# Where attention's token statistics, head rows and weight sums stand in the order of a two-layer decoder kernel

## The chip, the cores and the metric

The kernel runs on one core of a Trainium2 chip. A core has five engines with queues of their own: TensorE (PE, with weight loads shown as PEld), VectorE (DVE), ScalarE (ACT), GpSimd (POOL) and SyncE (SP, which here only issues transfers). They work side by side and wait for each other by semaphores. The metric is the device time of one execution in microseconds (us). The time of the kernel before is the median of three executions, 1449.32 us, of 1448.95 to 1450.97.

## The reference

Two layers over 528 tokens (16 learned ones and 512 of input) of width 1024. Layer 0 is an attention with forget gates, layer 1 a gated linear recurrence; each is followed by a gated feed-forward part with a short convolution. Cut to what matters here:

```python
def rms_norm(x, gain):
    return x * lax.rsqrt(jnp.mean(x * x, axis=-1, keepdims=True) + EPS) * gain

def fox_attention(h, norm_g, w_in, b_f, q_gain, k_gain, w_out):
    xn = rms_norm(h, norm_g)
    q, k, v, f_logit, o_gate = jnp.split(xn @ w_in, [D, 2 * D, 3 * D, 3 * D + H], axis=-1)
    q = rms_norm(q.reshape(B, L, H, hd), q_gain) * (hd ** -0.5)
    k = rms_norm(k.reshape(B, L, H, hd), k_gain)
    c = jnp.cumsum(jax.nn.log_sigmoid(f_logit + b_f), axis=1).transpose(0, 2, 1)
    # scores s = q.k + c_t - c_s, causal; softmax; o = p @ v
    o = o * jax.nn.sigmoid(o_gate)
    return o @ w_out

def conv_ffn(h, norm_g, w_gate, w_up, conv_w, conv_b, w_down):
    xn = rms_norm(h, norm_g)
    a = conv_b + causal_conv3(xn @ w_gate, conv_w)
    return (jax.nn.silu(a) * (xn @ w_up)) @ w_down
```

There are 16 heads of 64, so 8 pairs of heads, each pair 128 rows wide.

## The kernel before, in words

**Number form.** Activations and weights are kept as a sum of two parts, `hi` and `lo`. A product of 128 x 128 weights with 264 tokens is three matmuls, written by `proj_unit` at L250, L253 and L254. `weights` (L184) loads a weight tile into `raw` (two buffers), ACT makes `hi` (L200) and DVE `lo` (L126), with three buffers each. The factor 1/rms of a token is not multiplied into the activations: it is worked out beside the products and put on their results.

**Token statistics.** ACT squares the eight tiles of `h` and DVE adds them up to `ss` (L314, L318). `token_stats` (L345) lets PE sum `ss` over the partitions (L350, L352), and DVE takes the reciprocal root (`am`, `rsqn`, `rst`). In attention the sums are also needed as rows: PE makes them at L430, DVE copies them to `ssr` (L431), four transfers turn them into `et` (L434). `spread_rs` (L363) makes the row `rsb`, the factor for all partitions. All this is written ahead of the first products (L424 to L436).

**Stages of attention.** `stage_a(p)` makes q and k of pair p: 4 x 24 matmuls. For pair 0 the four products run side by side in the banks "p", "p", "c", "d"; other pairs take "p" banks, of which there are two (`bank`, L173; there are four "s" banks, one "c", one "d"). ACT squares and scales the results (L535, L536), PE sums the squares per head (L544), ACT copies them to `strow` (L545), four transfers bring them to `am2` (L549), where DVE adds `et` (L552), takes the reciprocal root and sends it back as `rows` (L559). `ssr`, `strow` and the forget logits `zr` are tiles of one tag with one buffer. `stage_n` multiplies the rows in (L573, L574), splits q and k and packs them into a slot (L600). `stage_f` makes the forget logits (L452, L453) and `forget` turns them into running sums on DVE, with a prefix over partitions on PE (L483); `decays` sends them into the slots (L612). `stage_v` makes values of two pairs with `values` (L268: L284, L291, L301). `stage_l` takes the log-sum-exp of the heads of a pair, one after the other, with `lse` (L730): five groups of scores (L744, L745, L747), the maxima on DVE (L757), exponentials on ACT, then a row that PE transposes (L779), DVE copies (L781) and transfers put into the slot (L784, L785). `stage_t` makes the attention itself. `stage_g` makes the output gate, `stage_p` a first part of the output projection.

**Order.** Stages are Python generators that yield a cost in us; `weave` interleaves them in proportion, `take` runs a part of one. The loop over p from -3 to 7 at L684 lays stage a of pair p+3, n of p+2, l of p+1 and t of p side by side. The order in which the instructions are written is not the order of issue: `tile.TileContext(nc, schedule_with_timeline_sim=True)` (L1432) sets the order of each engine at build time. `after(ins, prev)` (L94) adds an edge that keeps one instruction behind another in that order. On the chip each engine takes its queue in the order so fixed.

**Weight sums.** Most of the feed-forward part multiplies 2 x 2 blocks with seven products, for which sums of weight blocks are needed. `make_sums` (L211) is a generator: each step starts one or two sums, each by a load on SP and an adding transfer on POOL (L225, L226), into pieces of 512 columns of three shared tiles, two called `two` (four pieces each) and one called `one` (three). Six steps are taken in the output projection ahead of the feed-forward part (L727, L1096), then three in each `seven` (L1194, L1201, L1207). `plain` (L1239) makes the first pair of hidden tiles without sums.

Of the kernel before, what the change touches and what calls it, by code (L numbers as in the profile page):

```python
# [21 lines left out]
P = 128  # L22
D = 1024
KT = D // P
T = 528
# [57 lines left out]
class Builder:  # L83
# [158 lines left out]
    def proj_unit(self, ps, units, x, t0, tn, prev=None):  # L242
# [4 lines left out]
        for hi, lo, n in units:  # L247
            for i in range(n):
                xh, xl = (y[:, t0 : t0 + tn] for y in x[k])
                ins = mm(ps, hi[:, i, :], xh, start=k == 0, stop=False)  # L250
                if k == 0 and prev is not None:
                    self.after(ins, prev)
                mm(ps, hi[:, i, :], xl, start=False, stop=False)  # L253
                mm(ps, lo[:, i, :], xh, start=False, stop=k == total - 1)  # L254
                k += 1
                if k % 2 == 0:
                    yield 0.66
# [86 lines left out]

    def token_stats(self, segs, last=False, bank=None):  # L345

        nc = self.nc
        ps = (bank or self.misc)()[:, :12].rearrange("p (t c) -> p t c", c=2)
        for t, (t0, _, i0, _) in enumerate(segs):
            nc.tensor.matmul(ps[:, t, :], self.ss[:, t0 - i0 : t0 - i0 + P], self.onesd, start=True, stop=True)  # L350
        if last:
            nc.tensor.matmul(ps[:16, 5, :], self.ss[:, 512:528], self.onesd, start=True, stop=True)  # L352
        am = self.cp.tile([P, 6], F32, name="am", tag="am", bufs=2)
# [22 lines left out]
    def fox(self, ctx):  # L376
# [47 lines left out]
        start = partial(self.bank, "s")  # L424
        am, rs = self.token_stats(SEG0, True, start)
        et = sp.tile([64, 33], F32, name="et")
        ssr = s2.tile([2, T], F32, name="ssr", tag="strow", bufs=1)
        for t0, tn in full:
            sr = start()
            mm(sr[:2, :tn], self.onesd, self.ss[:, t0 : t0 + tn], start=True, stop=True)  # L430
            nc.vector.tensor_copy(ssr[:, t0 : t0 + tn], sr[:2, :tn])  # L431
        for g in range(4):
            t0, tn = full[g % 2]
            nc.sync.dma_start(et[16 * g : 16 * g + 16, :], ssr[:, t0 : t0 + tn].rearrange("r (j c) -> r j c", c=33))  # L434
        nc.vector.tensor_scalar(et, et, EPS, EPS, ALU.add, ALU.mult)
        self.spread_rs(rs, SEG0, start)  # L436
        rcol = [0, 1, 2, 3, 5]
# [71 lines left out]
        def stage_a(p):  # L509
# [16 lines left out]
            for w_, nm in ((0, "q"), (1, "k")):  # L526
# [4 lines left out]
                for i, (t0, tn) in enumerate(full):  # L531
                    ps = banks[i] if banks else bank()
                    if not banks:
# [11 lines left out]
            nc.scalar.copy(strow, pst[:, :264])  # L545
            yield 0.9
            am2 = self.tiny.tile([64, 33], F32, name="am2", tag="am2")
            for g in range(4):
# [68 lines left out]
        def stage_l(p):  # L617
            if p == 0:
                decays(0)
            for d in packs[p]:  # L620
                yield from self.lse(d, s2, identb, maskq)

# [61 lines left out]
        for p in range(-3, NPAIR):  # L684
            fill, cost = [], 0.0
            if p % 2 and 0 <= p + 1 < NPAIR:
                fill.append(vgen[p + 1])
                cost += half if p > 0 else 2 * half
            if p + 3 < NPAIR:
                fill.append(stage_a(p + 3))  # L690
# [29 lines left out]
        for i, m in enumerate([NEARLY, *range(NEARLY), *range(NEARLY + 1, KT)]):  # L720
# [4 lines left out]
            for step, _ in enumerate(out_proj(m, 6 if m < NEARLY else 0, KT, res)):  # L725
                if i > 1 and step == 0:
                    next(self.making)  # L727
# [111 lines left out]
    def hgrn(self, ctx):  # L839
# [254 lines left out]
        for m in range(KT):  # L1094
            if m > 1:
                next(self.making)  # L1096
# [10 lines left out]
    def ffn(self, ctx, layer, a0, o0):  # L1107
# [131 lines left out]
        def plain(j, out):  # L1239

            A, t = new_pair("A"), new_pair("t")[:, :, :n]
            for m in range(2):
                wg = [block(a[f"gu{layer}"][2 * j + m, 0, k]) for k in range(2)]
                for t0, tn in ga:
                    ps = self.bank("sp"[m])[:, :tn]
# [191 lines left out]
```

## Time and profile before

| | us |
|---|---|
| median of three executions | 1449.32 |
| profiled execution, whole | 1452.92 |
| its span, first to last instruction | 1451.1 |
| PE busy in it | 1420.7 |
| DVE busy | 1010.1 |
| ACT busy | 724.3 |

The difference of whole and span, 1.8 us, lies around the span. Times in a row of the timeline are the start from the beginning of the span and the length; a row may stand for several instructions (x10). What stands in brackets is how long the engine was idle before it, and what ended that. "PEclk" is the clock granted to PE, as a share of full speed: a matmul at a lower clock counts as busy and takes longer.

The first 350 us are attention, up to about 1100 us follow the first feed-forward part and the recurrence, the rest is the second feed-forward part.

### The profile page before, as it was taken

To read this page: it belongs to the slowest core of one execution; us is meant where nothing else is said; L and a number is where in the kernel's file an instruction comes from. 1 tells how busy PE (TensorE), PEld (TensorE's weight loads), DVE (VectorE), ACT (ScalarE), POOL (GpSimd) and SP (SyncE) were. 2 spreads that over 40 slices of the span, in tenths; PEclk is the share of its full clock that TensorE was granted. 3 is DMA by queue.
4 is the path that set the end of the run, shared out by engine and by line. 5 is a ranking of instruction groups with operands and counts; after the bars stand their busy time and mean duration, and the time that the engine had idled before them with its cause. 6 is when DMAs were issued, how large, how long until landed. Compare 5 with 4: busy or idle time off the path is not lost.

```text
span 1451.1 us, 29767 instructions
## 1 busy us (share of the span) xinstructions
PE 1420.7 (98%) x11368; PEld 1339.2 (92%) x11368; DVE 1010.1 (70%) x2282; ACT 724.3 (50%) x1528; POOL 164.3 (11%) x273
## 2 busy tenths in 40 slices
PE   7999999999899999999999999999999999999998
PEld 6898888899899999999999999999999899999997
DVE  6545455775698886767775667677656987777774
ACT  5356554663566554554543224333435665555551
POOL 4000000001012222221000000000100222221100
PEclk9999999999999999999999999999999999999999
DMA  4424344335659898886322202222643899989833
GB/s 161 120 63 134 76 124 123 89 99 150 182 138 232 231 238 203 205 214 165 97 61 87 88 2 88 61 72 74 170 122 84 206 256 220 237 214 222 203 90 101
DMA packets 105463, 206.90 MB, mean 143 GB/s; under 512 B 14168, under 2 KB 18008, under 8 KB 105320
## 3 DMA queue, kind: packets, MB, share of 16 engines
q1 hardware_dynamic: 82280, 163.05, 36.9%
q0 software_dynamic: 23040, 41.95, 17.5%
q8 instruction: 89, 1.46, 0.4%
q14 instruction: 54, 0.44, 0.1%
HBM read 168.53 MB, written 2.10 MB: 118 GB/s over the span
## 4 chain that ended last, share of the span: by engine, by line
PE 91%; DMA 4%; DVE 2%; ACT 2%; SPq 1%; issue 1%; DVEq 0%; ACTq 0%
PE pss L250 7%; PE pss L254 7%; PE pss L253 7%; PE psp L250 7%; PE psp L253 7%; PE psp L254 7%; PE psp L301 6%; PE psp L1183 5%; PE psp L1184 5%; PE psp L1185 5%; PE psd L1183 3%; PE psd L1184 3%; PE psd L1185 3%; PE psc L816 2%; PE pss L974 1%; PE psc L1183 1%
## 5 line engine op out<-in xcount | busy, mean ns | idle before, releaser
L126 DVE TENSOR_TENSOR lo<-raw,hi 128x512 fp32r<-128x512 f32 (+2 forms) x322 | 252.8, 790 | 79.8 <-ACT hi L1160 39.9
L250 PE MATMUL psp<-xhi,hi 128*128 128x264 f32 (+2 forms) x784 | 228.1, 292 | 6.2 <-ACT xhi L326 6.2
L253 PE MATMUL psp<-xlo,hi 128*128 128x264 f32 (+2 forms) x784 | 226.4, 289 | 0.0
L254 PE MATMUL psp<-xhi,lo 128*128 128x264 f32 (+2 forms) x784 | 225.9, 289 | 0.0
L1160 ACT CAST hi<-raw 128x512 fp32r<-128x512 f32 (+1 forms) x232 | 139.2, 604 | 170.4 <-PE pss L253 58.6
L253 PE MATMUL pss<-room,hi 128*128 128x264 f32 (+2 forms) x532 | 169.7, 320 | 0.0
L254 PE MATMUL pss<-room,lo 128*128 128x264 f32 (+2 forms) x532 | 168.8, 320 | 0.0
L250 PE MATMUL pss<-room,hi 128*128 128x264 f32 (+2 forms) x532 | 168.1, 320 | 0.0
L250 PEld LDWEIGHTS psp<-xhi,hi 128*128 128x128 f32 x784 | 149.9, 192 | 9.8 <-ACT xhi L326 6.2
L200 ACT CAST hi<-raw 128x1024 fp32r<-128x1024 f32 (+2 forms) x86 | 83.1, 968 | 145.0 <-PE psp L253 63.9
L253 PEld LDWEIGHTS psp<-xlo,hi 128*128 128x128 f32 x784 | 149.7, 191 | 2.2 <-issue 2.1
L254 PEld LDWEIGHTS psp<-xhi,lo 128*128 128x128 f32 x784 | 149.2, 191 | 2.0 <-issue 1.9
L1183 PE MATMUL psp<-xhi,hi 128*128 128x264 f32 (+1 forms) x480 | 136.4, 284 | 3.4 <-ACT hi L1160 2.7
L1185 PE MATMUL psp<-xhi,lo 128*128 128x264 f32 (+1 forms) x480 | 136.2, 284 | 0.9 <-DVE lo L126 0.9
L1184 PE MATMUL psp<-xlo,hi 128*128 128x264 f32 (+1 forms) x480 | 135.7, 283 | 0.0
L1160 ACT CAST hi<-two 128x512 fp32r<-128x512 f32 x118 | 72.9, 619 | 84.5 <-PE psd L1184 33.0
L254 PEld LDWEIGHTS pss<-room,lo 128*128 128x128 f32 x532 | 100.1, 189 | 6.3
L253 PEld LDWEIGHTS pss<-room,hi 128*128 128x128 f32 x532 | 100.2, 188 | 5.2
L250 PEld LDWEIGHTS pss<-room,hi 128*128 128x128 f32 x532 | 99.5, 188 | 4.2
L1307 DVE TENSOR_TENSOR h<-h,pss 128x264 f32<-128x264 f32 (+2 forms) x145 | 73.6, 508 | 36.3 <-PE pss L254 35.9
L1183 PEld LDWEIGHTS psp<-xhi,hi 128*128 128x128 f32 x480 | 90.7, 189 | 6.5 <-ACT hi L1160 4.0
L1183 PE MATMUL psd<-xfhi,hi 128*128 128x264 f32 (+1 forms) x320 | 90.8, 284 | 1.3 <-ACT hi L1160 0.7
(485 smaller groups left out, 3939.3 us busy)
## 6 DMA issues: line engine op xcount, KB each, us to landing
raw<-gu SPq DMA_DIRECT2D x136, 256.0 KB
two<-gu SPq DMA_DIRECT2D x118, 256.0 KB
raw<-dn SPq DMA_DIRECT2D x80, 256.0 KB
two<-gu POOLq DMA_DIRECT2D x58, 256.0 KB, 6.8
one<-gu SPq DMA_DIRECT2D x42, 256.0 KB
two<-two POOLq DMA_DIRECT2D x40, 256.0 KB, 5.0
pk<-stg SPq DMA_DIRECT2D x30, 264.0 KB
raw<-wqk SPq DMA_DIRECT2D x14, 512.0 KB
```

Of the source, the lines that this page charges most:

```text
L126: self.nc.vector.tensor_tensor(out, x, y, ALU.subtract)
L200: nc.scalar.copy(hi, raw)
L250: ins = mm(ps, hi[:, i, :], xh, start=k == 0, stop=False)
L253: mm(ps, hi[:, i, :], xl, start=False, stop=False)
L254: mm(ps, lo[:, i, :], xh, start=False, stop=k == total - 1)
L301: mm(ps[:tn, :256], y[:, t0 : t0 + tn], w, start=n == 0, stop=n == 23)
L816: ins = mm(o, v[:, j, 2 * (p % 2) + hd, :], w[hd][0], start=j == 0, stop=j == last)
L1160: nc.scalar.copy(hi, raw)
L1183: mm(ps, hi[:, k, :], xh, start=start and k == 0, stop=False, skip_group_check=not start)
L1184: mm(ps, hi[:, k, :], xl, start=False, stop=False, skip_group_check=not start)
L1185: mm(ps, lo[:, k, :], xh, start=False, stop=k == 3, skip_group_check=not start)
L1307: nc.vector.tensor_tensor(hv, hv, ps, ALU.add)
```

## The change

The diff does five things.

- `stats()` holds what stood ahead of the products: `token_stats`, the rows `ssr`, `et` and `spread_rs`. It is called in `stage_a(0)`, behind the copy to `strow` and ahead of the transfers to `am2`. Its matmuls on `ss` are kept behind `self.product`, the last matmul that `proj_unit` has written by then.
- The loop puts parts of pair 1 into the step p = -3: the products of pair 0 and their statistics per head, then the q products of pair 1, then the rest of pair 0 with `stats()`. The step p = -2 has the rest of pair 1 and half of the values. For this the products of pair 1 use "s" banks.
- `stage_l` writes the first group of scores of the second head ahead of the row of the first.
- Two steps of `make_sums` go from each output projection into `plain`, one for each of its two tiles.
- The bookkeeping of costs follows.

```diff
@@ proj_unit
-                mm(ps, lo[:, i, :], xh, start=False, stop=k == total - 1)
+                self.product = mm(ps, lo[:, i, :], xh, start=False, stop=k == total - 1)
@@ token_stats
-            nc.tensor.matmul(ps[:, t, :], self.ss[:, t0 - i0 : t0 - i0 + P], self.onesd, start=True, stop=True)
+            ins = nc.tensor.matmul(ps[:, t, :], self.ss[:, t0 - i0 : t0 - i0 + P], self.onesd, start=True, stop=True)
+            if prev is not None:
+                self.after(ins, prev)
...
@@ fox
-        am, rs = self.token_stats(SEG0, True, start)
         et = sp.tile([64, 33], F32, name="et")
-        ssr = s2.tile([2, T], F32, name="ssr", tag="strow", bufs=1)
...
-        self.spread_rs(rs, SEG0, start)
+        rs = None
+
+        def stats():
+
+            nonlocal rs
+            _, rs = self.token_stats(SEG0, True, start, self.product)
+            ssr = s2.tile([2, T], F32, name="ssr", tag="strow", bufs=1)
+            for t0, tn in full:
+                sr = start()
+                ins = mm(sr[:2, :tn], self.onesd, self.ss[:, t0 : t0 + tn], start=True, stop=True)
+                self.after(ins, self.product)
+                nc.vector.tensor_copy(ssr[:, t0 : t0 + tn], sr[:2, :tn])
...
+            self.spread_rs(rs, SEG0, start)
@@ stage_a
-                    ps = banks[i] if banks else bank()
+                    ps = banks[i] if banks else start() if p == 1 else bank()
...
             yield 0.9
+            if p == 0:
+                stats()
@@ stage_l
-            for d in packs[p]:
-                yield from self.lse(d, s2, identb, maskq)
+            one, two = (self.lse(d, s2, identb, maskq) for d in packs[p])
+            yield from chain(take(one, 1.8), take(two, 0.3), one, two)
@@ the loop over p
-                cost += half if p > 0 else 2 * half
-            if p + 3 < NPAIR:
+                cost += half
+            if p == -3:
+
+                first, second = stage_a(0), stage_a(1)
+                fill += [take(first, 10.6), take(second, 5.2), first]
+                cost += 18.1
+            elif p == -2:
+                fill += [second, take(vgen[0], half)]
+                cost += 7.5 + half
+            elif p + 3 < NPAIR:
@@ the output projections
-                if i > 1 and step == 0:
+                if i > NEARLY - 1 and step == 0:
                     next(self.making)
...
-            if m > 1:
+            if m > 3:
                 next(self.making)
@@ plain
                 wg = [block(a[f"gu{layer}"][2 * j + m, 0, k]) for k in range(2)]
+                next(self.making)
```

More of the change, by code (lines that the diff above doesn't have):

```diff
@@ L343, in rsqrt, with token_stats @@
         return y
-    def token_stats(self, segs, last=False, bank=None):
+    def token_stats(self, segs, last=False, bank=None, prev=None):
         nc = self.nc
@@ L349, in token_stats @@
         for t, (t0, _, i0, _) in enumerate(segs):
-            nc.tensor.matmul(ps[:, t, :], self.ss[:, t0 - i0 : t0 - i0 + P], self.onesd, start=True, stop=True)
+            ins = nc.tensor.matmul(ps[:, t, :], self.ss[:, t0 - i0 : t0 - i0 + P], self.onesd, start=True, stop=True)
+            if prev is not None:
+                self.after(ins, prev)
         if last:
-            nc.tensor.matmul(ps[:16, 5, :], self.ss[:, 512:528], self.onesd, start=True, stop=True)
+            ins = nc.tensor.matmul(ps[:16, 5, :], self.ss[:, 512:528], self.onesd, start=True, stop=True)
+            self.after(ins, prev)
         am = self.cp.tile([P, 6], F32, name="am", tag="am", bufs=2)
@@ L424, in fox @@
         start = partial(self.bank, "s")
-        am, rs = self.token_stats(SEG0, True, start)
         et = sp.tile([64, 33], F32, name="et")
-        ssr = s2.tile([2, T], F32, name="ssr", tag="strow", bufs=1)
[L428 to L435, printed above, removed]
-        self.spread_rs(rs, SEG0, start)
+        rs = None
[8 more added lines that the diff above has]
+                nc.vector.tensor_copy(ssr[:, t0 : t0 + tn], sr[:2, :tn])
+            for g in range(4):
+                t0, tn = full[g % 2]
+                nc.sync.dma_start(et[16 * g : 16 * g + 16, :], ssr[:, t0 : t0 + tn].rearrange("r (j c) -> r j c", c=33))
+            nc.vector.tensor_scalar(et, et, EPS, EPS, ALU.add, ALU.mult)
+            self.spread_rs(rs, SEG0, start)
         rcol = [0, 1, 2, 3, 5]
```

## The prediction

> **What bounds the kernel now.** I began with the busy table of the page.
>
> ```profile
> span 1451.1 us, 29767 instructions
> PE 1420.7 (98%) x11368; PEld 1339.2 (92%) x11368; DVE 1010.1 (70%) x2282; ACT 724.3 (50%) x1528; POOL 164.3 (11%) x273
> ```
>
> TensorE (PE) is busy for 1420.7 of 1451.1 us. The change takes no matmul away, so it can win only what PE loses: 30.4 us of idle time, and stretches in which it is busy at a lower clock. The waits of PE say where the idle time lies.
>
> ```profile
> PE psp L250 <- ACT xhi L326: 6.2, 1, 6.2
> PE pss L250 <- ACT hi L200: 3.5, 2, 2.2
> PE pss L350 <- DVE ss L318: 2.7, 1, 2.7
> PE pss L779 <- DVE rqq L342: 2.0, 1, 2.0
> PE psc L483 <- DVE tot L481: 1.4, 1, 1.4
> ```
>
> The columns are total us, times, longest. The first is the start of the kernel, which the change leaves alone. The second lies in the output projection of attention, beside the first weight sums. The third is the wait for the token statistics; the last two are waits inside attention. What they cost in clock stands in the table by stretches (length, then busy PE, PEld, DVE, ACT, POOL, then the granted clock, DMA share, GB/s):
>
> ```profile
> 20.00:25.00 5.00, 2.31 (x21) 2.05 (x20) 4.77 (x11) 4.66 (x10) 0.00 (x0) 1.00 0.56 197
> 25.00:30.00 5.00, 5.00 (x24) 2.77 (x22) 3.88 (x21) 0.95 (x3) 0.00 (x0) 0.66 0.01 4
> 185.00:190.00 5.00, 3.04 (x20) 2.51 (x16) 2.96 (x17) 1.28 (x4) 0.19 (x2) 0.62 0.65 215
> 190.00:195.00 5.00, 5.00 (x32) 4.89 (x32) 4.26 (x11) 3.23 (x12) 0.00 (x0) 0.70 0.34 107
> ```
>
> Behind the wait for the statistics the granted clock is 0.66 for 5 us, so 5 x 0.34 = 1.7 us more are lost. Behind the 2.0 us wait at L779 it is 0.62 and 0.70: 5 x 0.38 + 5 x 0.30 = 3.4 us.
>
> **The first edit: statistics behind products.** The timeline of PE, DVE and ACT at this place:
>
> ```profile
> 20.64 0.28 PE L254 MATMUL psd<-xhi,lo 128*128 128x264 f32 x1
> 23.61 1.28 PE L350 MATMUL pss<-onesd,ss 128*128 128x2 f32 x10 [2.69 <-DVE ss L318]
> 24.89 1.06 PE L430 MATMUL pss<-ss,onesd 128*2 128x264 f32 x4
> 25.77 1.05 PE L544 MATMUL psd<-sqq,hsel 128*32 128x264 f32 x2
> 28.59 0.93 PE L544 MATMUL psd<-sqq,hsel 128*32 128x264 f32 x6
> 29.68 0.29 PE L254 MATMUL psp<-xhi,lo 128*128 128x264 f32 x1
> 29.80 0.29 PE L250 MATMUL psp<-xhi,hi 128*128 128x264 f32 x1
> 22.05 1.51 DVE L318 TENSOR_TENSOR ss<-ss,sq 128x528 f32<-128x528 f32 x2
> 17.41 1.23 DVE L126 TENSOR_TENSOR lo<-raw,hi 128x1024 fp32r<-128x1024 f32 x1 [0.22 <-ACT hi L200]
> 25.43 0.51 ACT L536 ACTIVATE rawq<-psp,qg 128x264 f32<-128x264 f32 x1
> ```
>
> Pair 0's products end at 20.8. The sum of squares `ss` is ready at 23.5, and only then do the statistics run. Pair 1's q weights have been split since 18.6 (17.41 + 1.23), but its products need the two "p" banks, and ACT empties the last of these at 25.9. With the four "s" banks they need nothing that is late. 48 of them, 0.12 us apart (29.80 less 29.68), last 5.8 us: from 20.8 to 26.6, 3 us past the end of `ss`. So the wait of 2.69 us goes whole, and so does its cause for the low clock, 1.7 us. PE's work from 23.61 to 29.68 is otherwise the same, done in another order. One small thing is added: the eight L544 matmuls stand in two groups today, of which the first takes almost 1 us. Standing together they would be shorter by at most 0.7; apart, as now, by nothing. I take 0.3. **Sum of this edit: 2.7 + 1.7 + 0.3 = 4.7 us**, with 4.4 and 5.1 as its ends.
>
> Here a rule can be weighed. The Trainium skill, "TensorE: Matmul & The Clock Gate", section "What's actually happening", says that the array falls back to half its clock after at least one idle window of about 3.4 us. By that rule a gap of 2.7 us costs its own length, and the sum would be 2.7, not 4.4. The trace disagrees: 2.69 us of idle time stand ahead of a granted 0.66.
>
> Next, what moves behind it. `ssr`, `strow` and `zr` share one buffer, so that today `strow` of pair 0 waits for the copies out of `ssr`:
>
> ```profile
> 30.89 0.38 ACT L545 COPY strow<-psd 128x264 f32<-128x264 f32 x1 [4.94 <-DMA et<-ssr]
> 31.29 2.59 SPq L549 DMA_DIRECT2D am<-strow  x4
> 30.92 0.17 DVE L435 TENSOR_SCALAR et<-et 64x33 f32<-64x33 f32 x1 [1.67 <-DMA et<-ssr]
> 35.06 0.19 DVE L552 TENSOR_TENSOR am<-am,et 64x33 f32<-64x33 f32 x1 [2.38 <-DMA am<-strow]
> 27.22 0.41 DVE L431 COPY ssr<-pss 2x264 f32<-2x264 f32 x1
> ```
>
> After the change it is the other way round. `strow` can be copied at about 26.6, its four DMAs land 3.8 us after the copy's end (35.06 less 31.27), at 30.8, and `ssr` follows. From the last `ssr` copy to `et` are 3.3 us (30.92 less 27.63), so `et` comes at about 31.7 + 3.3 = 35.0 and the add of L552 at 35.2, where it is at 35.06 today. The two `ssr` copies wait on DVE in this time, and what is queued behind them there (the reciprocal root for `rst`, splits of weights) is late by up to 4 us. PE has pair 1's k products, the forget logits and half of the values to do meanwhile (48 + 32 + 42 matmuls of 0.12 us, 14.6 us). I cost it at nothing; without that cover it would be 0.1 to 4 us.
>
> **Is there work for a PE that is 4.7 us ahead?** The next thing that no product can hurry is the forget gate: `z` by DMA, a long chain on DVE, the prefix at L483, rows into `k1`, then the first scores.
>
> ```profile
> 54.24 0.26 DVE L464 TENSOR_SCALAR z<-z,vec 128x66 f32<-128x66 f32 x1 [3.95 <-DMA z<-zr]
> 66.31 0.19 DVE L552 TENSOR_TENSOR am<-am,et 64x33 f32<-64x33 f32 x1 [4.10 <-DMA am<-strow]
> 66.42 1.22 DVE L126 TENSOR_TENSOR lo<-raw,hi 128x1024 fp32r<-128x1024 f32 x1
> 68.11 0.38 PE L483 MATMUL psc<-tot,cst 128*128 128x2 f32 x2 [1.40 <-DVE tot L481]
> 74.54 0.17 PE L744 MATMUL pss<-pk 66*128 66x16 f32 x1
> 79.50 0.39 ACT L535 ACTIVATE sqq<-psp 128x264 f32<-128x264 f32 x1 [0.50 <-PE psp L254]
> ```
>
> The first scores start at 74.54, and 4.1 us of that chain are DVE standing at L552 until `am` lands. If none of this comes earlier, PE must find 4.7 us of other work before 74.5. Pair 3's q products are that work. Today they come after the scores begin (their first eviction is at 79.50). They are 48 matmuls of 0.12 us, 5.8 us, and their weights are split at 67.6 (66.42 + 1.22, behind the same stall). A PE that is 4.7 us early needs them at about 70. So the cover is 5.8 against 4.7, with a margin of 1.1 in amount and 2 in time. I take 0. One end is +6.4: without the cover the whole lead (4.7) goes and a slow stretch of 1.7 follows. The other is -1.4: the wait at L483 goes as well.
>
> **The second edit: rows of a head behind the next scores.** L779 transposes the row of a head when DVE has finished it. One of these waits:
>
> ```profile
> 187.10 0.44 PE L779 MATMUL pss<-identr,lr 128*128 128x128 f32 x1 [1.96 <-DVE rqq L342]
> 187.34 0.33 PE L744 MATMUL pss<-two 66*128 66x16 f32 x1
> 187.79 0.47 PE L744 MATMUL pss<-two 66*128 66x144 f32 x1
> ```
>
> One score group of the next head (187.34 to 187.79, 0.45 us) is put ahead of it, against 1.96 us. At the same time all stages shift against each other, so this wait may go whole or come back elsewhere. Its bounds are -5.4 (2.0 and its 3.4 of clock) and +3.7 (a new wait as long, with one stretch like that at 25). No row says which; I take 0.
>
> **The third edit: sums over more tiles.** Some steps of `make_sums` are only written later. The six steps ahead of the product loops make nine sums, in order into eight pieces of `two` and one of `one`; so a sum in `one` that adds a piece of `two` is a later one, written inside the loops of the feed-forward part.
>
> ```profile
> 335.12 0.80 SPq L225 DMA_DIRECT2D one<-gu  x2
> 368.07 0.86 POOL L226 DMA_DIRECT2D one<-two x1 [0.17 <-issue]
> 350.61 3.60 SPq L225 DMA_DIRECT2D two<-gu  x6
> 365.00:370.00 5.00, 3.59 (x28) 3.35 (x28) 4.28 (x10) 4.00 (x8) 1.72 (x2) 1.00 1.10 289
> 375.00:380.00 5.00, 5.00 (x34) 5.00 (x34) 4.03 (x6) 2.11 (x2) 0.00 (x0) 0.76 0.59 188
> ```
>
> The add at 368.07 is such a one, and it goes out in the middle of the output projection, as the loads into `one` do at 335, with attention still running. So a transfer goes out as soon as its buffer is free, and its place in the text only settles ties. The six at 350.61 go when the scores have left `two`, and they still would. I take 0. If they did wait, the `wo` weights would land sooner, and the waits of L250 for these (3.5) with the slow clock (5 x 0.24 = 1.2) could go: -4.7. If sums came late in the feed-forward part, I allow +2.0, a wait as long as that at L779.
>
> **The sum** is -4.7. The profiled execution took 1452.92 us (its span and 1.8 around it); 4.7 less is 1448.2. It lies 3.6 above the median of 1449.32, so the median becomes 1444.6. A measurement of this kernel tells about 0.2% from no change, 2.9 us.
>
> **Rivals.**
> 1. The forecast, the first edit alone: 1442 to 1446.4. Chance 0.40.
> 2. More goes: the wait at L779 too, or part of the waits of the projection. 1444.6 - 5.4 = 1439.2, and down to 1436. For it: the wait at L779 and its clock are the dearest single loss inside attention, and the order there is laid anew. Against it: nothing in the second edit covers 2 us of wait. Chance 0.20.
> 3. Within 0.2%. Either only the wait is saved and the clock falls all the same (1449.3 - 2.7 = 1446.6; 0.03 of the chance, since the row of 25 to 30 shows what the wait brings), or one new wait takes 2 to 5 us back. For it: any small shift between engines can make such a wait, and all stages of attention shift. Chance 0.26 in all. The rule of the Trainium skill, "TensorE: Matmul & The Clock Gate", section "What's actually happening", gives that 1446.6 as well.
> 4. Slower: PE runs out of work ahead of the first scores. The place is 70 to 75 us, and it decides itself when pair 3's q weights are split, or a bank for them is free, after 70. PE then waits, the 4.7 are gone, the low clock adds 1.7, and the scores come later by what `et` and `am` are late, up to 1.5: 1452.5. For it: L552 holds up both chains on DVE. Against it: 2 us of margin. Chance 0.14.
>
> That the third edit does nothing is part of the forecast. The range, 1437.5 to 1451.5, leaves out the far part of rival 2 and rival 4, some 0.19. Faster by over 0.2% is 1 and 2, 0.60; within 0.2%, 0.26; slower, 0.14.
>
> **What would show it.** In the profile after, L350 waits for nothing, stands behind pair 1's q products, and the clock in 25 to 30 is 1.00. `strow` is copied ahead of `ssr`. Between 66 and 76 PE goes on without a wait over 1.5 us, with pair 3's products ahead of the first scores. The sums' transfers start when `two` is free, as before. I am wrong if PE idles longer than 2 us between 28 and 100, or if a wait of 2 us with a slow stretch turns up in a new place of attention.

## The result, and the profile after

| | before | after |
|---|---|---|
| median, us | 1449.72 (1448.95 to 1450.97, 4 runs) | 1466.80 (1464.53 to 1470.29, 4 runs) |
| profiled execution, whole | 1452.92 | 1466.69 |
| its span | 1451.1 | 1464.9 |
| mean granted clock of PE in it | 0.994 | 0.988 |

The kernel after is slower: the ratio is 1.0119, with an interval of 1.0098 to 1.0141. The prediction was 1444.6, with a range of 1437.5 to 1451.5. It was wrong in sign. The page after, busy table:

```profile
span 1464.9 us, 29782 instructions
PE 1425.5 (97%) x11368; PEld 1341.2 (92%) x11368; DVE 1010.8 (69%) x2282; ACT 723.7 (49%) x1528; POOL 164.2 (11%) x273
```

The number of matmuls is the same. PE's idle time grew from 30.4 to 39.4 us (1464.9 less 1425.5), and its busy time by 4.8 us with the same work, a sign of a lower clock. So the loss has the form in which the prediction counted gains: idle time, and slow stretches. The table by stretches of the kernel after (length, busy PE, PEld, DVE, ACT, POOL, granted clock, DMA share, GB/s) shows where both lie:

```profile
20.00:25.00 5.00, 5.00 (x44) 5.00 (x43) 4.63 (x10) 4.84 (x12) 0.00 (x0) 1.00 0.45 156
25.00:30.00 5.00, 5.00 (x40) 3.47 (x38) 2.13 (x6) 3.12 (x8) 0.00 (x0) 1.00 0.01 2
...
75.00:80.00 5.00, 1.13 (x3) 0.56 (x3) 3.44 (x10) 2.20 (x4) 0.00 (x0) 0.97 0.06 8
80.00:85.00 5.00, 4.42 (x21) 3.28 (x22) 4.51 (x19) 1.75 (x4) 0.00 (x0) 0.50 0.31 66
...
110.00:115.00 5.00, 2.11 (x15) 1.44 (x15) 2.97 (x12) 2.58 (x9) 0.21 (x2) 0.89 0.35 73
115.00:120.00 5.00, 3.71 (x16) 2.85 (x15) 2.66 (x8) 3.15 (x13) 0.00 (x0) 0.50 0.89 198
120.00:125.00 5.00, 3.90 (x19) 3.13 (x20) 1.94 (x12) 1.52 (x7) 0.21 (x2) 0.50 0.27 56
...
380.00:385.00 5.00, 0.74 (x4) 0.54 (x4) 5.00 (x10) 2.50 (x4) 0.78 (x1) 0.85 1.09 259
385.00:390.00 5.00, 2.76 (x12) 2.76 (x13) 2.90 (x5) 3.25 (x4) 0.00 (x0) 0.50 0.43 136
```

The first two rows are the place that the change aims at, and it is clean: PE is busy all the time, at clock 1.00. The rest is new. From such rows a loss can be worked out for each stretch: idle is its length less busy PE, clock is its length times one less the clock. Summed by place over the first 420 us:

| place, us | before: idle + clock | after: idle + clock |
|---|---|---|
| 0 to 10, start | 6.2 + 0 | 6.7 + 0 |
| 20 to 30, token statistics | 2.7 + 1.7 | 0 |
| 65 to 135, first scores and first attention | 2.5 + 0 | 12.8 + 13.7 |
| 140 to 275, attention | 4.0 + 5.1 | 1.2 + 0 |
| 360 to 395, output projection | 5.6 + 1.7 | 8.6 + 3.4 |
| sum | 21.0 + 8.5 | 29.4 + 17.1 |

The sums differ by 17 us, the spans by 13.8. The wait of 4.4 us at the start is gone and so are 7.9 us in attention, but between 65 and 135 us 24 us more are lost. The timeline of the kernel after shows what the scores wait for there, and where PE stands from 75 us on:

```profile
28.54 0.38 ACT L555 COPY strow<-psd 128x264 f32<-128x264 f32 x1
32.93 0.76 DVE L440 COPY ssr<-pss 2x264 f32<-2x264 f32 x2 [0.99 <-DMA am<-strow]
37.51 0.19 DVE L564 TENSOR_TENSOR am<-am,et 64x33 f32<-64x33 f32 x1
57.47 5.77 SPq L612 DMA_DIRECT2D pk<-stg  x6
59.46 0.38 ACT L555 COPY strow<-psd 128x264 f32<-128x264 f32 x1 [2.01 <-PE psd L554]
63.34 3.90 SPq L561 DMA_DIRECT2D am<-strow  x4
68.95 0.37 ACT L467 COPY zr<-psc 16x264 f32<-16x264 f32 x1 [5.39 <-DMA am<-strow]
72.08 0.37 ACT L467 COPY zr<-psc 16x264 f32<-16x264 f32 x1 [0.75 <-PE psc L463]
76.02 0.36 PE L585 MATMUL psd<-rows,selr 128*128 128x264 f32 x1 [1.06 <-DMA rows<-yr]
76.92 0.26 DVE L474 TENSOR_SCALAR z<-z,vec 128x66 f32<-128x66 f32 x1
78.96 0.39 PE L585 MATMUL psd<-rows,selr 128*128 128x264 f32 x1 [1.68 <-DVE rawq L586]
93.46 2.82 SPq L624 DMA_DIRECT2D pk<-cneg  x4
96.28 0.25 PE L764 MATMUL pss<-pk 66*128 66x16 f32 x1 [1.44 <-DMA pk<-cneg]
```

In the kernel before, the same copies on ACT stood in another order:

```profile
38.92 0.37 ACT L457 COPY zr<-psc 16x264 f32<-16x264 f32 x1
48.14 0.37 ACT L457 COPY zr<-psc 16x264 f32<-16x264 f32 x1
56.59 0.38 ACT L545 COPY strow<-psd 128x264 f32<-128x264 f32 x1 [0.58 <-PE psd L544]
```

Read the first table from below. The first scores stand at 96.28; they stood at 74.54 before. They wait for the running sums of the forget gate (`cneg`), these for `z` (76.92, before 54.24), and `z` for the forget logits `zr`. The first copy into `zr` comes at 68.95, with ACT idle for 5.39 us ahead of it, released by the transfers `am<-strow`. Before, the two copies into `zr` were at 38.92 and 48.14, ahead of the second pair's copy into `strow` at 56.59. Now that copy (59.46) is ahead of them. `zr`, `strow` and `ssr` share one buffer: `zr` may only be written when `strow` has been read, its four transfers stand on SP behind the six packs (57.47 and 5.77 us), and so the forget gate starts 22 us late. The stand of PE from 75 to 82 us is another matter: its next matmuls there are those of L585, and they wait for the second pair's `rows`, which hang on the same four transfers, and for DVE.

The waits of PE after (total us, times, longest) name the later places:

```profile
PE pss L250 <- ACT hi L200: 7.5, 3, 4.7
...
PE pss L821 <- DMA pk<-lrow: 2.3, 1, 2.3
...
PE pss L799 <- DVE lr L126: 2.1, 1, 2.1
```

L799 and L821 are the rows of the heads and what needs them, in the stretch from 110 to 125. That the late scores leave no other work there is my reading; no row shows it. L250 is the output projection, which waits for its weights longer than before (3.5).

### The profile page after: what moved, and what is told of

The parts are those of the page before. It is cut to its first block, busy times and chain, and to the rows that moved or that the text cites. A ratio compares the mean times of both kernels' runs of the same rounds, so it can differ in the third digit from the quotient of the medians.

```text
span 1464.9 us, 29782 instructions
## 1 busy us (share of the span) xinstructions
PE 1425.5 (97%) x11368; PEld 1341.2 (92%) x11368; DVE 1010.8 (69%) x2282; ACT 723.7 (49%) x1528; POOL 164.2 (11%) x273
## 3 DMA queue, kind: packets, MB, share of 16 engines
q0 software_dynamic: 23040, 41.95, 17.4%
## 4 chain that ended last, share of the span: by engine, by line
PE 90%; DMA 4%; DVE 2%; ACT 1%; SPq 1%; issue 1%; DVEq 0%; ACTq 0%
PE pss L250 8%; PE pss L253 7%; PE pss L254 7%; PE psp L250 7%; PE psp L253 7%; PE psp L254 7%; PE psp L301 6%; PE psp L1203 5%; PE psp L1204 5%; PE psp L1205 5%; PE psd L1203 3%; PE psd L1204 3%; PE psd L1205 3%; PE psc L836 2%; PE pss L994 1%; PE psc L1203 1%
## 5 line engine op out<-in xcount | busy, mean ns | idle before, releaser
L250 PE MATMUL psp<-xhi,hi 128*128 128x264 f32 (+2 forms) x752 | 217.8, 291 | 7.6 <-ACT xhi L326 6.4
L253 PE MATMUL psp<-xlo,hi 128*128 128x264 f32 (+2 forms) x752 | 217.7, 290 | 0.0
L254 PE MATMUL psp<-xhi,lo 128*128 128x264 f32 (+2 forms) x752 | 216.8, 289 | 0.0
L253 PE MATMUL pss<-room,hi 128*128 128x264 f32 (+2 forms) x532 | 169.7, 320 | 0.0
L254 PE MATMUL pss<-room,lo 128*128 128x264 f32 (+2 forms) x532 | 168.8, 320 | 0.0
L250 PE MATMUL pss<-room,hi 128*128 128x264 f32 (+2 forms) x532 | 168.1, 320 | 0.0
L250 PEld LDWEIGHTS psp<-xhi,hi 128*128 128x128 f32 x752 | 143.2, 191 | 11.2 <-ACT xhi L326 6.4
L253 PEld LDWEIGHTS psp<-xlo,hi 128*128 128x128 f32 x752 | 143.4, 191 | 3.2 <-issue 3.1
L254 PEld LDWEIGHTS psp<-xhi,lo 128*128 128x128 f32 x752 | 143.1, 191 | 2.1 <-issue 1.4
L254 PEld LDWEIGHTS pss<-room,lo 128*128 128x128 f32 x532 | 100.1, 189 | 6.3
L253 PEld LDWEIGHTS pss<-room,hi 128*128 128x128 f32 x532 | 100.2, 188 | 5.2
L250 PEld LDWEIGHTS pss<-room,hi 128*128 128x128 f32 x532 | 99.5, 188 | 4.2
L1203 PEld LDWEIGHTS psp<-xhi,hi 128*128 128x128 f32 x480 | 90.7, 189 | 6.5 <-ACT hi L1180 4.0
```

What stands on the lines that cost most here:

```text
L254: self.product = mm(ps, lo[:, i, :], xh, start=False, stop=k == total - 1)
L1203: mm(ps, hi[:, k, :], xh, start=start and k == 0, stop=False, skip_group_check=not start)
```

## The experiments

My theory after the result was S: the shared buffer, which goes to the second pair's `strow` because that is now written ahead of `zr`. Its rivals were the second and third edits, and Q: SP's line between 55 and 75 us, which a TensorE that is ahead runs into. Ratios are to the kernel before, run on the same chip between the others, with 95% intervals.

**A buffer for `zr`.** The kernel after, with

```diff
-            zr = s2.tile([HF, T], F32, name="zr", tag="strow", bufs=1)
+            zr = s2.tile([HF, T], F32, name="zr", tag="rows")
```

> The changed kernel with one edit: zr, the forget logits, no longer shares the one buffer of ssr and strow, but takes a buffer of the tag rows, free since 31 us. Theory S (the shared buffer): in the changed kernel strow of pair 1 gets the buffer at 59.5 us, so zr can only be written at 69.0, when am has landed; the gate is some 22 us late and PE runs out of products at 75. Then here z reaches DVE at 50 to 57 us, the first scores start at 70 to 76, no wait of PE over 2 us is left between 65 and 135, and the time falls by 12 to 17 us, to 1449 to 1455. Theory W (work): the products moved ahead are missing before the scores, whatever zr does. Then z comes earlier, but PE still idles by 4 us or more between 65 and 135, and the time stays at 1458 or above.

Measured: 1455.85 us, ratio 1.0034 (1.0021 to 1.0047). The timeline, and the table by stretches:

```profile
43.60 0.37 ACT L467 COPY zr<-psc 16x264 f32<-16x264 f32 x1
59.98 0.38 ACT L555 COPY strow<-psd 128x264 f32<-128x264 f32 x1 [1.19 <-PE psd L554]
71.20 1.04 ACT L200 CAST hi<-raw 128x1024 fp32r<-128x1024 f32 x1 [5.78 <-DMA raw<-wv]
72.96 0.39 PE L250 MATMUL psp<-xhi,hi 128*128 128x264 f32 x1 [2.28 <-ACT rawk L546]
```

```profile
70.00:75.00 5.00, 2.72 (x18) 2.51 (x17) 2.65 (x12) 1.99 (x4) 0.00 (x0) 0.87 0.34 132
75.00:80.00 5.00, 5.00 (x36) 4.71 (x35) 2.38 (x7) 2.50 (x9) 0.00 (x0) 0.79 0.03 6
```

The copies into `zr` come at 43.60 and 49.66, `z` at 53.2, the first scores at 76.28. One tile's tag gives back 11 of the 17 us. Theory S is right on `z`, but not on the waits: PE still idles for 6.9 us between 65 and 135, more than the 4 us that theory W asked for, and the time lies between the ranges of the two. Where the 11 us come from can be read by place. From 90 to 135 us the loss is 7.4 in place of 17.3; from 65 to 90 it is 8.0 in place of 9.1. So the shared buffer cost its time behind the late scores, and a loss of nearly the same size between 65 and 90 stays without it. That rest, 5 us to the kernel before and 11 to the forecast, stays. One part of it is in the rows: ACT stands for 5.78 us until the weights `wv` have landed, and copies that would free PE's banks stand behind it, so that PE waits 2.28 us and runs at a lower clock after that.

**The order instead of the buffer.** The kernel after, with the two parts of the step p = -2 exchanged:

```diff
-                fill += [second, take(vgen[0], half)]
+                fill += [take(vgen[0], half), second]
```

> The changed kernel with the two parts of step p = -2 exchanged: the half of the values first, the rest of pair 1 behind it, so that the statistics per head of pair 1 are written behind the forget logits. The buffer stays shared. Theory S (the shared buffer, taken by the wrong tile): zr is written before strow of pair 1, z reaches DVE at 50 to 57 us, the first scores start at 72 to 80, and the time is 1450 to 1458, near the 1455.85 of the kernel with a buffer for zr. Theory W (products moved ahead are missing later): the first scores stay late or PE idles as long, 1462 or above.

Measured: 1453.54 us, 1.0028 (1.0016 to 1.0041), inside the range of theory S. The buffer is shared as before, and `zr` comes at 38.88 and 49.31, `strow` of the second pair at 61.59, the scores at 76.73. So it is the place in the written order that hands the buffer on, and changing that alone is worth as much as a second buffer.

**The same buffer in the kernel before.** One line, as in the first experiment:

> The kernel before with zr in a buffer of its own; nothing else. In it zr is first evicted at 38.92, ahead of the first pair's strow copy that it shares the buffer with (56.59). Theory S (the kernel after lost its 13 us in the forget gate because strow of the second pair came to stand ahead of zr): here zr is ahead anyway, so nothing is gained, z at 53 to 55, first scores at 74 to 76, time 1447 to 1452. Rival (the shared buffer cost time in the kernel before too, and a buffer for zr is worth something in itself): the second half of zr, 48.14, comes over 1 us earlier and the time falls below 1446.

Measured: 1450.02 us, 1.0000 (0.9988 to 1.0011). The order of the instructions is the same on all engines. The buffer cost nothing as long as `zr` came first.

**The edits one by one.** The kernel after without its second and third edit (rows of a head and sums as in the kernel before):

```diff
-            one, two = (self.lse(d, s2, identb, maskq) for d in packs[p])
-            yield from chain(take(one, 1.8), take(two, 0.3), one, two)
+            for d in packs[p]:
+                yield from self.lse(d, s2, identb, maskq)
...
-                if i > NEARLY - 1 and step == 0:
+                if i > 1 and step == 0:
...
-            if m > 3:
+            if m > 1:
```

> The changed kernel with its second and third edits undone: lse of a pair's heads one after the other as before, and the steps of the weight sums where they were. Theory S: the loss is in the first edit; the first scores start at 94 to 98 us as in the changed kernel, and the time is 1459 to 1468. If the rows behind the next scores cost the time (theory L), the waits between 100 and 130 go and it falls to 1455 or below. If the sums cost the 3.8 us that the output projection lost, the shift between the end of attention and the statistics of the feed-forward part goes back to that of before and 3 to 4 us with it.

Measured: 1471.57 us, 1.0140 (1.0123 to 1.0157), above the 1459 to 1468 of theory S; `z` comes at 76.97 and the scores at 96.35. The first edit by itself makes the whole loss and a little more. The third edit alone, in the kernel before:

> The kernel before with the third edit alone: two steps of the weight sums go from each output projection into plain. As predicted (a transfer goes when its buffer is free): same to 0.2%, 1447 to 1452, the loads into two at 349 to 354 us as before. Theory P (the sums cost the output projection its 3.8 us): 1452.5 to 1455, with the wo weights later between 354 and 378.

Measured: 1448.82 us, 0.9988 (0.9977 to 1.0000), nothing or a little gained. The transfers into `two` go out together again, as the row at 350.61 did:

```profile
347.24 3.82 SPq L225 DMA_DIRECT2D two<-gu  x6
```

The second edit alone, in the kernel before:

> The kernel before with the second edit alone: the first scores of the second head stand ahead of the row of the first. As predicted (one group of scores covers 0.45 us, the rest is chance): 1444 to 1453. Theory L (it is what makes PE wait in attention): 1454 or above, with new waits at the transposes of the rows.

Measured: 1457.65 us, 1.0045 (1.0029 to 1.0062), as theory L had the time. But no new wait at the transposes made it: the wait that the edit is put in front of is still there (2.3 us at the transpose of a row), and the table by stretches shows the loss in the output projection, with no change made there:

```profile
370.00:375.00 5.00, 2.25 (x9) 1.64 (x8) 5.00 (x10) 3.04 (x5) 0.00 (x0) 0.50 0.89 214
375.00:380.00 5.00, 3.19 (x15) 3.19 (x16) 3.99 (x6) 3.27 (x4) 0.00 (x0) 0.53 0.52 156
```

The first edit alone with a buffer for `zr`:

> The first edit alone, with a buffer of its own for zr; second and third edit undone. If the second edit costs here what it cost the kernel before (6.5 us), the time is 1447 to 1452; if its cost there was chance of that one order, 1453 to 1460. Wait by wait: with the gate on time, PE idles at most 5 us between 65 and 90, as in the kernel with all three edits and the buffer, since that loss (ACT behind a late load of wv) belongs to the first edit.

Measured: 1458.63 us (1453.51 to 1461.51), 1.0056 (1.0037 to 1.0074). Scores at 74.04. Without the second and third edit this is no faster than with them (1.0034 above), so I read the 6.5 us that the second edit cost in the kernel before as a matter of that order, not as a price of the edit. Now the core of the first edit by itself: the kernel before with `stats()` behind pair 1's q products in "s" banks, and the values where they were.

```diff
+            if p == -3:
+                first, second = stage_a(0), stage_a(1)
+                fill += [take(first, 10.6), take(second, 5.2), first]
+                cost += 18.1
+            elif p == -2:
+                fill.append(second)
+                cost += 7.5
```

> The kernel before with the statistics behind pair 1's q products (on s banks) and nothing else: the values stay whole in step p = -1, heads and sums as before, buffer shared. As I predicted for the first edit: no wait at the statistics, clock 1.00 in 25 to 30, zr ahead of strow of pair 1 as before, and 1443 to 1449. If a PE that is ahead only meets the same late transfers (theory Q: the queue on SP, with the packing of pair 0 and am ahead of the next weights, bounds 55 to 75 us), the gain is given back before the first scores and the time is 1449 to 1455.

Measured: 1458.93 us, 1.0060 (1.0044 to 1.0076), above the ranges of the prediction and of theory Q. Here the start does what it should, and goes on doing so: `z` at 49.45 in place of 54.24, the first scores at 70.20 in place of 74.54. Then the lead melts. The first result of attention (`po`) is copied at 107.5, 2.2 us ahead of the kernel before; the last at 357.68, 5.7 us behind it. With the third edit added:

> The kernel of the run before with the third edit besides. The sums alone gave 0.1%; if the two add up, this is 1 to 3 us below the run before. It is the version that could beat both kernels: 1441 to 1448 by the prediction, 1447 to 1453 by theory Q.

Measured: 1456.53 us, 1.0044 (1.0027 to 1.0061), again above both ranges. Nothing is lost at one place; it goes in pieces. The first of them, in the kernel with the statistics alone:

```profile
70.00:75.00 5.00, 4.80 (x29) 4.59 (x30) 2.52 (x6) 3.54 (x12) 0.00 (x0) 0.71 0.04 6
75.00:80.00 5.00, 3.93 (x26) 3.26 (x25) 2.76 (x8) 2.05 (x7) 0.11 (x1) 0.95 0.31 90
80.00:85.00 5.00, 4.38 (x30) 3.88 (x31) 3.48 (x11) 3.61 (x10) 0.11 (x1) 0.73 0.14 40
```

PE waits 0.2, 1.1 and 0.6 us here, and loses 1.5, 0.3 and 1.4 to the clock. Summed by place as in the table above, 65 to 135 us costs 9.5 us (2.5 before), 180 to 260 costs 12.2 (140 to 275 before: 9.1), 360 to 385 costs 8.4 (7.3). So in this profile 4.4 are won and 11 given back.

**SP's line.** Theory Q was tried by giving the packs another queue, in three kernels:

```diff
-                dma = lambda o, i: nc.sync.dma_start(o.bitcast(F32), i.bitcast(F32))
+                dma = lambda o, i: nc.gpsimd.dma_start(o.bitcast(F32), i.bitcast(F32))
```

The kernel before with it:

> The kernel before, with the six pack transfers of each pair (pk<-stg) issued on POOL's queue in place of SP's; nothing else. A control for the two runs beside it. In the kernel before the six stand on SP from 55.52 to 61.60, and behind them the four am transfers (61.70) and the next weights (65.22, 67.67); ACT's next cast of weights is at 68.68. Theory Q (SP's line between 55 and 75 us is what a TensorE that is ahead runs into): the am transfers and the weights go out 5 to 6 us earlier, the 1.4 us that TensorE stands between 65 and 70 us goes, time 1447 to 1450. Rival R (what comes after is fitted to where TensorE is, and any shift loses something later): the 1.4 us is made up later, 1449 to 1453. Rival T (transfers issued by POOL land later than those issued by SP): first scores later than 75.5, time above 1451.

The kernel after with a buffer for `zr` and with it:

> The kernel after, with zr in a buffer of its own (as in e1_zr_own, 1455.85) and the six pack transfers of each pair on POOL's queue. Theory Q: without the 5.85 us of packs ahead of them the am transfers go out at about 58 in place of 63.54 and the weights of the values at about 61.5 in place of 67.14, ACT's cast of them (71.20) starts 4 to 6 us earlier, and TensorE's loss between 70 and 90 us (4.6 idle and 3.4 at a lower clock) falls below 3: time 1448 to 1451.5. Rival R: the loss between 70 and 90 may fall, but at least as much is lost at another place, 1454 to 1457. Rival T: first scores later than 77, time above 1457.

The kernel with statistics and sums and with it:

> The kernel before with the token statistics behind the first pair's products of q and the sums spread (as in e8_stats_sums, 1456.53), and the six pack transfers of each pair on POOL's queue. Its first scores came 4.3 us ahead of those of the kernel before, and the lead was gone by the end of the first half. Theory Q: the weights of the values (66.75) go out about 5 us earlier, the lead of 4 us is still there at the first po copy (105 or earlier, 107.5 without the edit), and the time is 1446 to 1451, so that it may beat the kernel before. Rival R: lead at the first po copy below 3 us, new gaps behind it, time 1455 to 1458. Rival T: first scores later than 72, time above 1457.

Measured: 1463.04 (1.0084, 1.0060 to 1.0107), 1472.21 (1.0144, 1.0127 to 1.0161) and 1470.15 (1.0131, 1.0116 to 1.0146). Q's forecast fails in all three: each is 12 to 16 us worse than without the edit. The first scores come at 75.29, 82.10 and 76.56, so rival T's sign (late scores) is met in the second and the third. In the third one the four small transfers do go out 3.5 us earlier (59.75; 63.25 in e8_stats_sums), and land later. Timeline and stretches of e11_pk_stats:

```profile
59.75 3.68 SPq L561 DMA_DIRECT2D am<-strow  x4
73.36 0.19 DVE L564 TENSOR_TENSOR am<-am,et 64x33 f32<-64x33 f32 x1 [9.78 <-DMA am<-strow]
76.56 0.35 PE L764 MATMUL pss<-pk 66*128 66x16 f32 x1 [7.14 <-DMA pk<-cneg]
```

```profile
65.00:70.00 5.00, 4.42 (x37) 4.21 (x35) 0.00 (x0) 1.95 (x4) 0.00 (x0) 1.00 1.02 216
70.00:75.00 5.00, 0.00 (x0) 0.00 (x0) 1.50 (x10) 0.00 (x0) 0.00 (x0) 0.77 0.18 51
```

The weights now go out ahead of them (57.28; 66.75 in e8_stats_sums) and the packs beside them; the DMA engines are full from 60 to 70 (shares 1.04 and 1.02), the last pack lands at 72.69, and the 8 KB are used at 73.36, 9.9 us after they were issued (59.75 + 3.68). Whether the queue or the traffic beside it delays them, these runs don't separate: they took the packs off SP's line, but let everything run at once. DVE stands on them for 9.78 us with `cneg` queued behind, and PE stands for all of 70 to 75. In the second one PE waits 7.3 us for the transfers of `rows`. In the first, the kernel before with this edit, the scores are on time and it is another matter: at over 1700 of the 11368 places in PE's order another matmul stands, and the time goes at 115 to 125, 250 to 265 and 375 to 390.

**Fewer bytes.** That left two theories: D, the full DMA engines are what a TensorE that is ahead meets, and O, each edit lays the order of all instructions anew and opens gaps elsewhere. The six packs of a pair move 1.6 MB. Three of them stay on their partitions, and can be copies on POOL, which is idle there:

```diff
-                dma(d["pk"][0:64, 0:2, :], stg[sl, 0:3:2, :])
-                dma(d["pk"][0:64, 2:4, :], stg[sl, 0:4:3, :])
-                dma(d["pk"][64:128, 2:4, :], stg[sl, 1:3, :])
+                own = lambda o, i: nc.gpsimd.tensor_copy(o, i.bitcast(F32))
+                (own if hd == 0 else dma)(d["pk"][0:64, 0:2, :], stg[sl, 0:3:2, :])
+                (own if hd == 0 else dma)(d["pk"][0:64, 2:4, :], stg[sl, 0:4:3, :])
+                (own if hd == 1 else dma)(d["pk"][64:128, 2:4, :], stg[sl, 1:3, :])
```

In the kernel before, in that with statistics and sums, and in the kernel after with a buffer for `zr`:

> The kernel before, where three of the six pack transfers of each pair, those whose source and target stand on the same partitions, are copies on POOL; three transfers stay on SP. A control for the two runs beside it. The 16 DMA engines are 0.64, 0.84 and 0.56 busy in the three stretches of 5 us from 55 to 70 in the kernel before. Theory D (it is the transfers' time that holds TensorE there): half of the 1.6 MB goes, the share from 60 to 65 falls below 0.6, the am transfers go out at about 59 in place of 61.70, the 1.4 us that TensorE stands at 65 to 70 goes; time 1447 to 1451. Theory O (the whole order of the instructions is laid anew after any edit, and gaps of TensorE of 2 us with their stretch at the lower clock open at other places): DMA share falls just so, but the time is above 1453.

> The kernel of e8_stats_sums (token statistics behind the first pair's products of q, sums spread, 1456.53) with the same three transfers as copies on POOL. There the DMA engines were 0.98 busy from 60 to 65, and TensorE stood 0.9 us from 70 to 75 and 1.7 us from 75 to 80. Theory D: share from 60 to 65 below 0.75, first scores at 68 to 70, TensorE's loss from 65 to 90 below 1.5, the lead of 4 us over the kernel before is still there at the first po copy (below 106); time 1445 to 1451. Theory O: the share falls, the lead is there at the first scores, and is lost behind them in gaps at other places; time 1453 to 1460.

> The kernel after with zr in a buffer of its own (e1_zr_own, 1455.85) and the same three transfers as copies on POOL. Theory D: loss of TensorE from 70 to 90 below 3 in place of 8, time 1447 to 1451.5. Theory O: the same loss from 70 to 90 or less, but gaps elsewhere that take it back; time 1453 to 1460. In each run the sum of TensorE's idle time and of its time lost to the lower clock in the first 420 us should account for the time to within 2 us: the span less that sum was 1417.4 to 1421.6 in all runs so far.

Measured: 1447.02 (0.9979, 0.9967 to 0.9990), 1452.94 (1.0014, 1.0001 to 1.0026) and 1452.68 (1.0016, 1.0004 to 1.0029). By the ratios each is some 3 to 4 us below the same kernel without the copies (0.21, 0.30 and 0.18%), with the first edit and without it. The stretches of e13_copy_before:

```profile
60.00:65.00 5.00, 5.00 (x44) 5.00 (x43) 4.55 (x18) 2.46 (x3) 0.44 (x1) 1.00 0.33 84
65.00:70.00 5.00, 5.00 (x43) 5.00 (x42) 4.62 (x22) 2.32 (x5) 0.00 (x0) 1.00 0.60 197
...
185.00:190.00 5.00, 5.00 (x44) 4.70 (x44) 2.40 (x8) 2.25 (x8) 0.00 (x0) 1.00 0.33 116
```

The DMA share from 60 to 65 falls from 0.84 to 0.33, the 1.4 us of waiting at 65 to 70 goes, and so does the wait at 185. This is the fastest kernel measured, 0.2% below the kernel before. There theory D holds. In the two with the first edit it does not: between 65 and 90 us e14_copy_stats still loses 7.7 us to idle and clock (D: below 1.5; 6.0 without the copies), and between 70 and 90 e15_copy_zr loses 6.4 (D: below 3; 8.0 without). Their gain comes at other places. And the first edit still costs 6 us beside the copies (1452.94 against 1447.02), so these transfers are at most a part of what takes its lead. Last, these copies with the third edit:

> The two edits that lay at or below the kernel before, together: three of the six pack transfers of each pair as copies on POOL (e13_copy_before, 0.9979 of the kernel before) and the weight sums spread over more tiles (e3_sums_only, 0.9988); token statistics, values and rows as in the kernel before. If the two are independent: 0.9967, 1445.5 to 1447.5. Theory O: each edit lays the order anew, so that the two together are not the sum of the two; anything from 1445 to 1452, and the sum of idle and clock loss in the first 420 us accounts for it.

Measured: 1449.10 us, 0.9987 (0.9977 to 0.9998). The two gains do not add up to 0.9967; with the intervals of all three runs that is hardly clear of noise.

**One account for all.** In each of the 18 profiles I summed PE's idle time and its clock loss over the first 420 us, and took the sum from the span:

| kernel | span | idle + clock | span less these |
|---|---|---|---|
| before | 1451.1 | 21.0 + 8.5 | 1421.6 |
| after | 1464.9 | 29.4 + 17.1 | 1418.5 |
| e1_zr_own | 1453.9 | 19.9 + 13.6 | 1420.4 |
| e7_stats_only | 1455.1 | 22.7 + 13.7 | 1418.7 |
| e11_pk_stats | 1468.0 | 31.9 + 17.1 | 1419.0 |
| e12_zr_own_before | 1446.6 | 17.4 + 10.2 | 1418.9 |
| e13_copy_before | 1448.8 | 17.6 + 10.2 | 1421.0 |

All 18 lie between 1417.2 and 1421.6. So the rest, the products and what is lost behind 420 us, is the same to 4.4 us whatever is edited; the kernels differ by the gaps that PE meets in attention and the output projection, and by the slow stretches there. One caution: e12_zr_own_before issues on every engine in the order of the kernel before, and yet its profile is 4.5 us shorter and has its slow stretches at partly other places. So a single gap or slow stretch in one profile can be what two executions of the same order differ by, and the verdicts above rest on the medians.

## Why the prediction was wrong

**The first edit at the start: right.** L350 waits for nothing, the clock from 25 to 30 is 1.00, and `strow` of pair 0 is copied ahead of `ssr`, all as foretold. The 4.4 us are gone. The eight sums per head take 1.28 us of PE in place of 1.98. But they still stand in two groups (26.74 and 27.84), and before they ran at the low clock that the 1.7 us already counts, so the 0.3 for standing together is not shown. `et` comes at 37.3 in place of 35.0, and the cover that I named for it held: PE waits for nothing there.

**"What moves behind it": the step that failed.** I wrote there that `ssr`, `strow` and `zr` share one buffer, followed it for pair 0, where `strow` and `ssr` change places, and priced it at nothing, with 0.1 to 4 us as the price without cover. I did not ask who has the buffer next. The step p = -2 now writes the rest of pair 1, and with it that pair's `strow`, ahead of the half of the values beside which the forget logits run. So `zr` got the buffer fourth instead of third, behind a copy, a line of six packs and four transfers. That made the forget gate 22 us late. Of the kernel's 17 us it explains 11 to 13: a buffer of its own and the exchanged order each take that back, and the same buffer does nothing where `zr` was first.

**"Is there work for a PE that is 4.7 us ahead?"** I asked this with the forget gate fixed at its old time. In the kernel after it was 22 us later, and the cover of 5.8 us, pair 3's q products, was used up by 75. Where the gate is on time, its chain moved up along with PE (`z` 4.8 us earlier in e7_stats_only). So the step held up to the first scores, better than I had it, and said nothing of what followed.

**The sum.** Even with the buffer out of the way, -4.7 did not appear: +5 in e1_zr_own, +10 in e7_stats_only. The sum rested on a silent term, that a lead of PE at 30 us is still there at 400. The runs show the lead lost in gaps at other places. Halving the bytes of the packs is worth some 3 us with the first edit and without, but with it not at the place where the DMA engines were full; it leaves 6 us of the first edit's cost. What makes these gaps open where they do was not settled. That any re-ordering costs is no rule either: the sums and the copies gave a little.

**The second edit, taken as 0 between -5.4 and +3.7:** by itself 1.0045, or +6.5 us, outside these bounds. It did not take the wait away, and the price was paid in the output projection, where I had not looked for it. Beside the first edit it cost nothing that the runs show (1.0034 with it and the third edit, 1.0056 without). **The third, taken as 0:** 0.9988, and its transfers wait for their buffer, as I had it.

**The rivals.** Rival 4 had the sign and nearly the place (PE runs out of work ahead of the first scores; it stands from 75 on). Its cause was not pair 3's q weights, whose products ran before that, nor the 1.5 us of `et` and `am`, and its price, 1452.5, was 14 us short: the greater part of the loss lies behind the late scores. Both signs that I gave for being wrong were met: PE idles for 3.87 us from 75 to 80, in waits of up to 1.7 us, and waits of over 2 us with a slow stretch stand at a new place, L799 and L821.

## What to carry to other kernels

When a stage moves, list for each tag with one buffer all its users in the order in which they will be written, up to the last of them; the cost is that of whoever stands behind a long reader, not of the stage that moved. Ask what each new place puts ahead of the longest chain that no other work can hurry (here the forget gate), and price that chain's delay first. In this kernel, whose TensorE is 98% busy and whose order is laid anew at each build, a gain at one place was no forecast for the whole: the median moved by -3 to +21 us after edits that should have been worth a few us at one spot.

## What the runs showed of the hardware

- The traces record two granted clocks only, 1.00 and 0.50. In all 18 profiles each spell at 0.50 lasts 3.41 us or two to five times that, but for the last one, which the end of the program cuts. A spell so costs 1.7 us or a multiple (half its length): the 8.5 and 17.1 us of the account above are 5 and 10 times 1.7. The values between in the tables are averages over 5 us.
- The record of the clock begins only at 10 to 12 us, and the tables show 1.00 ahead of it. In the kernel before, L250, L253 and L254 stand 0.22 us apart until 12.1 us and 0.12 us behind that, so by my estimate the start loses 2 to 3 us more, in which the account above sees nothing.
- A gap of PE of 2.28 us (e1_zr_own, at 72.96) was enough for a lower clock behind it: 0.87 and 0.79 in the two stretches quoted there. In the kernel before, the gap of 1.40 us at L483 (68.11) has none:

```profile
65.00:70.00 5.00, 3.60 (x30) 3.39 (x29) 3.38 (x15) 1.32 (x3) 0.00 (x0) 1.00 0.56 166
70.00:75.00 5.00, 5.00 (x44) 4.92 (x43) 2.59 (x9) 1.53 (x5) 0.00 (x0) 1.00 0.14 49
```

  In e12_zr_own_before, in the same order, PE idles there for 1.60 us, and has one:

```profile
65.00:70.00 5.00, 3.40 (x24) 3.19 (x23) 4.27 (x21) 1.71 (x3) 0.00 (x0) 0.89 0.63 210
70.00:75.00 5.00, 5.00 (x36) 5.00 (x34) 1.60 (x3) 0.77 (x2) 0.00 (x0) 0.77 0.05 9
```

  The length of a single gap does not settle it: in e14_copy_stats a spell of 6.83 us at 0.50 begins at 250.8 behind two gaps of 0.55 and 0.43 us (248.27 and 250.51). What does was not tested.

- In the kernel after the clock stayed at 0.50 from 115 to 130, though PE was busy for 3.7 to 5 of each 5 us there; the two waits of over 2 us there are the 2.08 us at L799, which end at 113.94, and the 2.30 us at L821, which end at 121.01. It is one spell of 17.07 us, from 113.9.
- In e11_pk_stats, where the DMA share was 1.02 for most of the time, four transfers of 8 KB in all were used 9.9 us after the last was issued. In the kernel before, where it was 0.84 and then 0.56, they were used 1.2 after it (issued until 65.12, used at 66.31).
- POOL's three copies of 64 x 1056 take 3.75 us together (e13_copy_before); the three transfers that they replace held SP for about 3 (six in 6.08).
